# Segment mean: data of the last rows in halves, and looks, ids and counts of the last rows moved forward

## Chip, cores, metric

One core of one Trainium2 chip. The metric is the time of one execution in device microseconds (us). Each ratio below is given with its 95% interval and the chip it was measured on. "Row" is one of 90 slices of 875 values per partition; VectorE is DVE in the profile, ScalarE is ACT, GpSimd is POOL, the sync engine is SP.

## The reference

```python
n = 10_000_000; num_segments = 10000
data = np.random.randn(n).astype(np.float32)
segment_ids = np.sort(np.random.randint(0, num_segments, n))

sums = np.zeros(num_segments); counts = np.zeros(num_segments)
np.add.at(sums, segment_ids, data)
np.add.at(counts, segment_ids, 1)
return sums / np.maximum(counts, 1)
```

The ids are sorted, so a row of one partition holds at most a few segments. The kernel reads a sparse sample of the ids ("probes"), works out per row where the boundary must lie (the "look"), gathers only the 175 ids around it, and from them gets the exact boundary.

## The kernel before

Four engines share a row. GpSimd issues the gathers of a group of six rows after VectorE's look has computed their addresses. ScalarE adds up the gathered ids of a row (`add_ids`, which gives `KK`, the boundary) and the row's data (`total`). VectorE sums the data before the boundary (`split`), and in between does the small work on counts and outputs that `after[r]` holds. The data come in tiles of two rows from the sync engine.

```python
def x_sum(r):                       # how many rows ahead the ids of row r are added
    return 6 if r < HALVES else 3   # HALVES = 66

def load_data(t):                   # tile t = rows 2t and 2t+1, one transfer of 875 KB
    d = dpool.tile([P, 2 * L], FP32, name="data_t")
    a, b = 2 * t * L, min(2 * (t + 1) * L, D)
    c = b if t < NT - 1 else a + L  # only the last tile goes in two transfers
    nc.sync.dma_start(out=d[:, 0 : c - a], in_=data_p[:, a:c])
    if c < b:
        nc.sync.dma_start(out=d[:, c - a : b - a], in_=data_p[:, c:b])

def add_ids(r):                     # ScalarE, KK[r] = sum over 175 ids
    if r >= HALVES:
        nc.scalar.activation(out=junk_a, in_=gt32[:, r % RING, 0 : 2 * W : 2], func=ACT.Identity,
                             scale=-1.0, bias=YY[:, r : r + 1], accum_out=KK[:, r : r + 1])
        if r == NR - 1:             # the correction for the short last row
            nc.scalar.activation(out=KK[:, r : r + 1], in_=KK[:, r : r + 1], func=ACT.Identity, bias=tl)
        return
    ...
def total(r):                       # ScalarE, sum of the row
    nc.scalar.activation(out=junk_t[:, 0:n], in_=d, func=ACT.Copy, accum_out=t_of(r, r + 1))
def split(r):                       # VectorE, sum of the row before the boundary
    nc.vector.scalar_tensor_tensor(out=junk_v[:, 0:n], in0=iota[:, 0:n], scalar=KK[:, r : r + 1], in1=d,
                                   op0=ALU.is_lt, op1=ALU.mult, accum_out=A[:, r : r + 1])
... # cut: looks, windows, keys, tables, checks
put(NR - 4, counts(RM, R2), 99)     # VectorE, 7 small instructions, need KK of rows 72 to 89
put(NR - 1, sums(RM, R2, False) + spread(...) + total_of(add, OUT[:, C2:NO]), 99)

for r in range(-X_PIECE - X_DATA, NR):
    ...
    while r >= -1 and gs < NR and gs <= r + x_sum(gs):
        add_ids(gs)
        gs += 1
    if r >= 0:
        total(r)
        split(r)
        for f in after[r]:
            f()
```

Of the kernel before, what the change touches and what calls it, by code (L numbers as in the profile page):

```python
# [19 lines left out]
L = 875  # L20
S = 175
K = L // S
NR = 90
# [7 lines left out]
X_PIECE = 15  # L31
PIECE = 2
X_DATA = 26
X_LOOK = 9
RING = 18
HALVES = 66
NO = 79
# [5 lines left out]
R2 = NR + 4  # L43
RM = 72
RE = 84
C1, CA, C2 = 41, 64, 50
# [71 lines left out]
def kernel(  # L118
# [6 lines left out]
    nc = tc.nc  # L125
# [15 lines left out]
    ctx.enter_context(tc.manual_schedule())  # L141

    def x_sum(r):
        return 6 if r < HALVES else 3


    pr = cpool.tile([P, NR + 1, K], I64, name="pr")
# [7 lines left out]
    bounds = [0]  # L155
# [10 lines left out]
    def load_data(t):  # L166
        d = dpool.tile([P, 2 * L], FP32, name="data_t")
        a, b = 2 * t * L, min(2 * (t + 1) * L, D)
        c = b if t < NT - 1 else a + L
        nc.sync.dma_start(out=d[:, 0 : c - a], in_=data_p[:, a:c])  # L170
        if c < b:
            nc.sync.dma_start(out=d[:, c - a : b - a], in_=data_p[:, c:b])
        tiles[t] = d
# [9 lines left out]
    def view(ap, dims):  # L183
        return bass.AP(ap.tensor, ap.offset, [list(ap.ap[0])] + dims)
# [90 lines left out]
    def first_look(g):  # L275

        a, b = bounds[g], bounds[g + 1]
        n = b - a
        far = fpool.tile([P, n], FP32, name="far", bufs=3)
        last = b == NR  # L280
        v = nc.vector

        def s1():
            v.tensor_reduce(out=SG[:, a:b], in_=pr32[:, a:b, 0 : 2 * K : 2], axis=AX.X, op=ALU.add)  # L284

        def s2():
            v.scalar_tensor_tensor(  # L287
                out=ST[:, a:b], in0=VI[:, a + 1 : b + 1], scalar=float(K), in1=SG[:, a:b],
                op0=ALU.mult, op1=ALU.subtract,
            )  # L290

        def s3():
            v.tensor_scalar(out=far, in0=ST[:, a:b], scalar1=0.0, scalar2=FAR, op0=ALU.is_equal, op1=ALU.mult)  # L293

        def s4():
            v.tensor_add(out=ST[:, a:b], in0=ST[:, a:b], in1=far)  # L296

        def s5():
            for c, d, w in [(a, b - 1, S), (b - 1, b, TAIL)] if last else [(a, b, S)]:
                v.scalar_tensor_tensor(  # L300
                    out=IDX[:, c:d], in0=ST[:, c:d], scalar=float(w), in1=wb[:, c:d], op0=ALU.mult, op1=ALU.add
                )
            if a < HALVES:
                v.scalar_tensor_tensor(  # L304
                    out=YY[:, a:b], in0=ST[:, a:b], scalar=float(K + 1), in1=SG[:, a:b], op0=ALU.mult, op1=ALU.add
                )
            else:
                v.tensor_add(out=YY[:, a:b], in0=ST[:, a:b], in1=VI[:, a + 1 : b + 1])
            if last:
                v.tensor_scalar(  # L310
                    out=tl, in0=ST[:, NR - 1 : NR], scalar1=-1.0, scalar2=float(TAIL - S),
                    op0=ALU.add, op1=ALU.mult,
                )
            gather(g)

        return [s1, s2, s3, s4, s5]

    def gather(g):
        for r in range(bounds[g], bounds[g + 1]):
            nc.gpsimd.indirect_dma_start(  # L320
                out=GT[:, r % RING, :],
                out_offset=None,
                in_=ids2d[:],
                in_offset=bass.IndirectOffsetOnAxis(ap=IDX[:, r : r + 1], axis=0),
                bounds_check=N - W,
                oob_is_err=False,
            )
# [58 lines left out]
    pb = cpool.tile([P, NO - C2, R2 - RM], FP32, name="pb")  # L386
# [153 lines left out]
    def check_columns():  # L540

        return [
            lambda i=i, q=q, r=r: nc.scalar.activation(
                out=bad[:, NC + 5 + i : NC + 6 + i], in_=VI[:, r : r + 1], func=ACT.Relu, scale=q,
                bias=edge[:, i : i + 1],
            )
            for i, (q, r) in enumerate(((-1.0, R1), (-1.0, RM), (1.0, RM - 1)))
        ]
# [19 lines left out]
    def counts(a, b):  # L568


        n = b - a
        ps = fpool.tile([P, n], FP32, name="ps")
        ct = fpool.tile([P, n], FP32, name="ct")

        def s1():
            nc.vector.tensor_add(out=ps, in0=KK[:, a:b], in1=QQ[:, a:b])  # L576

        def s2():
            nc.vector.tensor_tensor_scan(  # L579
                out=PS[:, a + 1 : b + 1], data0=ps, data1=ps, initial=PS[:, a : a + 1],  # L580
                op0=ALU.max, op1=ALU.max,
            )

        def s3():
            nc.vector.tensor_sub(out=ct, in0=ps, in1=PS[:, a:b])  # L585

        def s4():
            nc.vector.reciprocal(out=ct, in_=ct)  # L588

        def s5():  # L590
            c = min(b, NR)
            nc.vector.tensor_mul(out=RB[:, a:c], in0=BT[:, a:c], in1=ct[:, 0 : c - a])  # L592
            if c < b:
                nc.vector.tensor_mul(out=RB[:, c:b], in0=MX[:, 0 : b - c], in1=ct[:, c - a : n])  # L594

        return [s1, s2, s3, s4, s5]
# [75 lines left out]
    def table(m0, m1, t):  # L672
        def s1():
            nc.vector.tensor_tensor(
                out=sel[:, m0:m1], in0=sel[:, m0:m1], in1=windows(RF, m0, m1), op=ALU.mult
            )

        def s2():
            nc.vector.tensor_reduce(
                out=t[:, 7 * m0 : 7 * m1].rearrange("p (m k) -> p m k", k=7), in_=sel[:, m0:m1],  # L680
                axis=AX.X, op=ALU.add,
            )

        return [s1, s2]

    def place(c0, c1, t, outs):
        def s1():
            n = c1 - c0
            nc.vector.tensor_tensor(
                out=shf[:, c0:c1, 0:ND], in0=view(t[:, c0 : c0 + 1], [[1, n], [1, ND]]),  # L690
                in1=view(dm[:, 0:1], [[0, n], [1, ND]]), op=ALU.mult,
            )

        def s2():
            for a, b, d, o in outs:
                nc.vector.tensor_reduce(out=o, in_=shf[:, a:b, 0:d], axis=AX.X, op=ALU.add)

        return [s1, s2]

    def pick(e, o, c0, n, a, b):  # L700

        w = b - a

        def s1():
            c = min(b, NR)
            e.tensor_scalar(
                out=KL[:, a - R1 : c - R1], in0=VI[:, a:c], scalar1=sp[:, 0:1], scalar2=None, op0=ALU.subtract
            )
            if c < b:
                e.tensor_scalar(  # L710
                    out=KL[:, c - R1 : b - R1], in0=V[:, c:b], scalar1=sp[:, 0:1], scalar2=None,
                    op0=ALU.subtract,
                )

        def s2():
            k, j = view(KL[:, a - R1 : a - R1 + 1], [[0, n], [1, w]]), view(jj[:, c0 : c0 + 1], [[1, n], [0, w]])
            if e is nc.vector:
                e.tensor_tensor(out=o, in0=k, in1=j, op=ALU.is_equal)
            else:
                e.tensor_tensor(out=o, in0=k, in1=j, op=ALU.subtract)  # L720
                e.tensor_scalar(out=o, in0=o, scalar1=0.0, scalar2=None, op0=ALU.is_equal)  # L721

        return [s1, s2]
# [26 lines left out]
    NG = len(GROUPS)  # L750
    NT = (NR + 1) // 2
# [7 lines left out]
    def put(r, steps, every=1):  # L759
        for i, f in enumerate(steps):  # L760
            after[r + i // every].append(f)
# [6 lines left out]
            put(a - 1, second_look(a, b))  # L768
    for g in range(HEAD, NG):
        if g < NG - 1:  # L770
            put(max(bounds[g] - X_LOOK, 0), first_look(g), 5)

    def mixed(p, q):
        out = []
# [8 lines left out]
    def sentinel():  # L783
# [11 lines left out]
    t = table(M1, NT1 // 7, tax)  # L795
# [12 lines left out]
    CF = 7 * H1 - ND + 1  # L808
    put(50, place(0, CF, tab, [(0, CF, ND + 1, OUT[:, 0:CF])]))
    put(65, place(CF, T1, tab, [(CF, C1, ND + 1, OUT[:, CF:C1]), (C1, T1, ND + 1, xa[:, 0 : T1 - C1, RM - R1])]))  # L810
    look = bounds[NG - 1] - X_LOOK - 2
    put(46, check_frame(), 2)
    put(66, check_windows())
    put(65, pick(nc.vector, pa[:, :, 0 : RM - R1], C1, CA - C1, R1, RM))
    put(66, check_columns(), 99)
    put(68, pick(nc.gpsimd, pb[:, :, 0 : RE - RM], C2, NO - C2, RM, RE), 99)
    put(look, first_look(NG - 1), 99)
    put(RM - 3, counts(R1, RM), 2)
    put(look, pick(nc.gpsimd, pb[:, :, RE - RM :], C2, NO - C2, RE, R2), 99)
# [5 lines left out]
    put(RM + 3, spread(R1, RM, pa[:, :, 0 : RM - R1], xa[:, :, 0 : RM - R1], CA - C1, nc.gpsimd)[1:])  # L825
    put(83, total_of(xa[:, 0 : C2 - C1, :], OUT[:, C1:C2])
        + total_of(xa[:, C2 - C1 :, :], add[:, 0 : CA - C2, nb]))
    put(NR - 4, counts(RM, R2), 99)
    put(NR - 1, sums(RM, R2, False) + spread(RM, R2, pb, add[:, :, 0:nb], NO - C2) + total_of(add, OUT[:, C2:NO]), 99)
    assert max(after) <= NR - 1  # L830

    def ahead(p):
        return X_PIECE if p == 0 else p - 1 - 2 * max((p - 4) // 4, (p - X_PIECE - 1) // 2)
# [3 lines left out]
    gs = 0  # L837
    for r in range(-X_PIECE - X_DATA, NR):
        while pnext < NR and pnext <= r + ahead(pnext) + X_DATA:
            n = GROUPS[0] if pnext == 0 else PIECE  # L840
# [4 lines left out]
            pnext += n  # L845
        while nt < NT and 2 * nt <= r + X_DATA:
            load_data(nt)
            nt += 1
        if r == -X_DATA:
            nc.scalar.dma_start(  # L850
# [48 lines left out]
```

## Time and profile before

| | before |
|---|---|
| median of 4 runs | 187.98 us (187.78 to 190.61; the 190.61 was slow) |
| span of the profiled run | 186.0 us |
| busy: VectorE, ScalarE, GpSimd | 137.3, 120.5, 99.2 us |
| bytes moved | 54.62 MB |
| row 84 starts on VectorE | 171.48 us |
| last reduction ends | 181.83 us |

Until about 172 us the transfers are full; from row 84 on VectorE works without a gap. The lines that show this stand in the prediction. In the timeline lines here and below the columns are: start in us, duration in us, engine, line of the program, operation, what it writes and reads, shapes, count, and in brackets the idle time just before with what ended it. VectorE's `junk_v` is a row's split, ScalarE's `junk_t` a row's total, ScalarE's `junk_a` a row's ids.

### The profile page before, as it was taken

Reading aid. Unit: us, or ns where it says so; the run is one execution under the profiler, and the core shown is the slowest. Engines: PE = TensorE matmul, PEld = TensorE weight load, DVE = VectorE, ACT = ScalarE, POOL = GpSimd, SP = SyncE. Lnnn points to the kernel's source line nnn. Section 1 sums busy time; section 2 is a strip of 40 time slices with the busy share of each in tenths; the row PEclk is TensorE's granted clock in tenths of the full one; section 3 lists DMA queues with packets and bytes.
Section 4 is the critical chain, followed back from the end, with each engine's and each line's share of the span. In section 5 each row is a group of like instructions: output and inputs, shape, how many; then the busy total and the mean of one; then the engine's idle time right before and its main releaser. Section 6 shows DMA issues by size and latency. Waiting matters only on the chain. (4 is left out here: it accounts for less than half of the span.)

```text
span 186.0 us, 1471 instructions
## 1 busy us (share of the span) xinstructions
PE 2.2 (1%) x8; PEld 1.9 (1%) x8; DVE 137.3 (74%) x414; ACT 120.5 (65%) x371; POOL 99.2 (53%) x119
## 2 busy tenths in 40 slices
PE   0000000000002000000000000000000000110000
PEld 0000000000001000000000000000000000110000
DVE  7410089999278994955799998766689979887991
ACT  8001487933899186962846939387569769998920
POOL 4677767057843757166173572827517857782000
DMA  6999999999999999999999999999999999999100
GB/s 28 324 250 269 267 283 281 327 333 318 325 321 323 336 331 309 332 327 325 309 297 327 342 319 319 312 306 335 335 286 299 336 351 404 405 399 396 50 0 10
DMA packets 70612, 54.62 MB, mean 294 GB/s; under 512 B 60464, under 2 KB 61032, under 8 KB 70599
## 3 DMA queue, kind: packets, MB, share of 16 engines
q1 hardware_dynamic: 64667, 40.50, 74.6%
q0 software_dynamic: 5760, 14.01, 24.4%
q14 instruction: 13, 0.11, 0.2%
q10 hardware_dynamic: 172, 0.00, 0.1%
HBM read 56.59 MB, written 0.04 MB: 305 GB/s over the span
## 5 line engine op out<-in xcount | busy, mean ns | idle before, releaser
L320 POOL DMA_INDIRECT GT<-in_segment_ids_dram,IDX x90 | 90.0, 1001 | 66.6 <-issue 23.5
L361 DVE SCALAR_TENSOR_TENSOR junk_v<-iota,q,data_t 128x875 bf16<-128x875 f32 x90 | 100.7, 1119 | 16.9 <-DMA data_t<-in_data_dram 14.6
L356 ACT ACTIVATE junk_t<-data_t 128x875 bf16<-128x875 f32 x90 | 83.7, 930 | 10.1 <-DMA data_t<-in_data_dram 9.8
L338 ACT ACTIVATE junk_a<-GT 128x175 f32<-128x175 int32 x66 | 22.1, 334 | 46.6 <-DMA GT<-in_segment_ids_dram,IDX 33.6
L356 ACT ACTIVATION_READ_ACCUMULATOR junk_t<-data_t 128x1 f32 x90 | 15.4, 171 | 0.0
L284 DVE TENSOR_REDUCE SG<-pr 128x6 f32<-128x30 int32 x15 | 2.7, 179 | 15.3 <-DMA pr<-in_segment_ids_dram 15.3
L331 ACT ACTIVATE junk_a<-GT,YY 128x175 f32<-128x175 int32 x24 | 9.9, 412 | 0.0
L338 ACT ACTIVATION_READ_ACCUMULATOR junk_a<-GT 128x1 f32 x66 | 9.3, 141 | 0.0
L361 DVE DVE_READ_ACCUMULATOR junk_v<-iota,q,data_t 128x1 f32 x90 | 7.4, 82 | 0.0
L345 DVE SCALAR_TENSOR_TENSOR q<-YY,G 128x6 f32<-128x6 f32 x11 | 1.7, 156 | 7.2 <-ACT junk_a L338 7.2
L331 ACT ACTIVATION_READ_ACCUMULATOR junk_a<-GT,YY 128x1 f32 x24 | 4.6, 192 | 0.0
L186 ACT ACTIVATE GT<-q 128x3150 int32<-128x3150 f32 x1 | 3.0, 2991 | 0.0
L293 DVE TENSOR_SCALAR far<-ST 128x6 f32<-128x6 f32 x15 | 2.6, 171 | 0.5
L300 DVE SCALAR_TENSOR_TENSOR IDX<-ST,wb 128x6 int32<-128x6 f32 (+2 forms) x16 | 2.6, 165 | 0.5
L287 DVE SCALAR_TENSOR_TENSOR ST<-pr,SG 128x6 f32<-128x6 int32 x15 | 2.5, 166 | 0.5
L296 DVE TENSOR_TENSOR ST<-ST,far 128x6 f32<-128x6 f32 x15 | 2.5, 165 | 0.5
L721 POOL TENSOR_SCALAR pb<-pb 128x348 f32<-128x348 f32 (+1 forms) x2 | 2.1, 1028 | 0.2
L560 PE MATMUL misc<-bads,ones 128*128 128x1 f32 x2 | 0.6, 362 | 102.2 <-ACT badj L552 102.2
L186 ACT ACT_TABLE_LOAD x1 | 1.3, 1283 | 0.7 <-PEq L883 0.7
L304 DVE SCALAR_TENSOR_TENSOR YY<-ST,SG 128x6 f32<-128x6 f32 x11 | 1.7, 158 | 0.0
L560 PEld LDWEIGHTS misc<-bads,ones 128*128 128x128 f32 x2 | 0.5, 310 | 102.3 <-ACT badj L552 102.3
L720 POOL TENSOR_TENSOR pb<-KL,jj 128x348 f32<-128x348 f32 (+1 forms) x2 | 1.5, 733 | 0.2
(126 smaller groups left out, 46.0 us busy)
## 6 DMA issues: line engine op xcount, KB each, us to landing
data_t<-in_data_dram SPq DMA_DIRECT2D x44, 875.0 KB, 10.0
GT<-in_segment_ids_dram,IDX POOLq DMA_INDIRECT x90, 6.3
pr<-in_segment_ids_dram SPq DMA_DIRECT2D x41, 10.0 KB, 7.4
data_t<-in_data_dram SPq DMA_DIRECT2D x1, 437.5 KB, 18.4
data_t<-in_data_dram SPq DMA_DIRECT2D x1, 125.0 KB
out_dram<-OUT SPq DMA_DIRECT2D x1, 36.6 KB
pr<-in_segment_ids_dram SPq DMA_DIRECT2D x1, 31.0 KB, 4.0
snt<-in_segment_ids_dram ACTq DMA_DIRECT2D x1, 1.0 KB
```

The source lines that it names most:

```text
L186: nc.scalar.activation(out=gt32[:, :, 0 : 2 * W : 2], in_=view(q5[:, 0, 0:1], [[0, RING], [0, W]]), func=ACT.Copy)
L284: v.tensor_reduce(out=SG[:, a:b], in_=pr32[:, a:b, 0 : 2 * K : 2], axis=AX.X, op=ALU.add)
L287: v.scalar_tensor_tensor(out=ST[:, a:b], in0=VI[:, a + 1 : b + 1], scalar=float(K), in1=SG[:, a:b], op0=ALU.mult, op1=ALU.subtract,)
L293: v.tensor_scalar(out=far, in0=ST[:, a:b], scalar1=0.0, scalar2=FAR, op0=ALU.is_equal, op1=ALU.mult)
L296: v.tensor_add(out=ST[:, a:b], in0=ST[:, a:b], in1=far)
L300: v.scalar_tensor_tensor(out=IDX[:, c:d], in0=ST[:, c:d], scalar=float(w), in1=wb[:, c:d], op0=ALU.mult, op1=ALU.add)
L320: nc.gpsimd.indirect_dma_start(out=GT[:, r % RING, :], out_offset=None, in_=ids2d[:], in_offset=bass.IndirectOffsetOnAxis(ap=IDX[:, r : r ...
L331: nc.scalar.activation(out=junk_a, in_=gt32[:, r % RING, 0 : 2 * W : 2], func=ACT.Identity, scale=-1.0, bias=YY[:, r : r + 1], accum_out=K ...
L338: nc.scalar.activation(out=junk_a, in_=gt32[:, r % RING, 0 : 2 * W : 2], func=ACT.Copy, accum_out=g_of(r, r + 1),)
L356: nc.scalar.activation(out=junk_t[:, 0:n], in_=d, func=ACT.Copy, accum_out=t)
L361: nc.vector.scalar_tensor_tensor(out=junk_v[:, 0:n], in0=iota[:, 0:n], scalar=KK[:, r : r + 1], in1=d, op0=ALU.is_lt, op1=ALU.mult, accum_ ...
L721: e.tensor_scalar(out=o, in0=o, scalar1=0.0, scalar2=None, op0=ALU.is_equal)
```

## The change

Intent: let each row of the last tiles start when its own data are there, and clear the way for it: looks earlier so that the ids are there, ids five rows ahead, and the counts that need the last ids two rows earlier, so that less stands behind the last data. (`bounds[NG - 1]` is 84.)

```diff
+FINE = 78
     def x_sum(r):
-        return 6 if r < HALVES else 3
+        return 6 if r < HALVES else 3 if r < bounds[NG - 1] else 5
-        c = b if t < NT - 1 else a + L
+        c = b if 2 * t < FINE else a + L
-            put(max(bounds[g] - X_LOOK, 0), first_look(g), 5)
+            put(max(bounds[g] - X_LOOK - 2 * (g == NG - 2), 0), first_look(g), 5)
-    look = bounds[NG - 1] - X_LOOK - 2
+    look = bounds[NG - 1] - X_LOOK - 3
-    put(68, pick(nc.gpsimd, pb[:, :, 0 : RE - RM], C2, NO - C2, RM, RE), 99)
+    put(66, pick(nc.gpsimd, pb[:, :, 0 : RE - RM], C2, NO - C2, RM, RE), 99)
-    put(NR - 4, counts(RM, R2), 99)
+    put(NR - 6, counts(RM, R2), 99)
```

One line added near the top shifts all line numbers by one: L577 after is L576 before, L337 is L336.

## The prediction

> **What bounds the kernel now.** I began with the page's slices, to see which resource is full in which stretch.
>
> ```profile
> DVE  7410089999278994955799998766689979887991
> ACT  8001487933899186962846939387569769998920
> POOL 4677767057843757166173572827517857782000
> DMA  6999999999999999999999999999999999999100
> GB/s 28 324 250 269 267 283 281 327 333 318 325 321 323 336 331 309 332 327 325 309 297 327 342 319 319 312 306 335 335 286 299 336 351 404 405 399 396 50 0 10
> ```
>
> A slice is 4.65 us. The transfers are full from the second slice to the 37th, that is to about 172 us, and no compute engine is full over that time. So the transfers set the pace until 172 us; then VectorE works alone. Moving loads about cannot shorten the first part: the bytes stay the same. What can be won lies in the 14 us behind it, and the chain that ended last says of what they consist:
>
> ```profile
> 173.88 0.09 issue
> 173.98 1.14 DVE junk_v L361 x2
> ...
> 176.33 1.06 DVE junk_v L361 x2
> ...
> 180.98 0.85 DVE OUT L739
> ```
>
> VectorE never pauses here up to 181.83 us; the output transfer takes the rest to 186.0. To find where this unbroken run starts, I read the timeline of the end backwards, counting rows from row 89 (the only one 250 wide, at 178.59 us):
>
> ```profile
> 162.45 1.13 DVE L361 SCALAR_TENSOR_TENSOR junk_v<-iota,q,data_t 128x875 bf16<-128x875 f32 x1 [0.59 <-ACT junk_a L331]
> 165.36 1.13 DVE L361 SCALAR_TENSOR_TENSOR junk_v<-iota,q,data_t 128x875 bf16<-128x875 f32 x1 [0.53 <-DMA data_t<-in_data_dram]
> 168.70 1.13 DVE L361 SCALAR_TENSOR_TENSOR junk_v<-iota,q,data_t 128x875 bf16<-128x875 f32 x1 [0.97 <-DMA data_t<-in_data_dram]
> 171.48 1.13 DVE L361 SCALAR_TENSOR_TENSOR junk_v<-iota,q,data_t 128x875 bf16<-128x875 f32 x1 [0.23 <-ACT junk_a L331]
> 174.20 0.29 ACT L336 ACTIVATE q<-q,tl 128x1 f32<-128x1 f32 x1
> 175.03 0.18 DVE L576 TENSOR_TENSOR ps<-q,QQ 128x22 f32<-128x22 f32 x1
> ```
>
> These are rows 78, 80, 82 and 84, each the first of a two-row tile, each behind an idle gap; then ScalarE's last id instruction (row 89) and the start of the last counts. The trace's completion records put the ends of these four tiles at about 162.4, 165.23, 168.58 and 171.35 us, just before each start. So I read the two gaps charged to ScalarE as waits for data as well: ids of rows 78 and 84 were added three rows earlier. From row 84 at 171.48 there is no gap. **The time is therefore the start of row 84 plus a fixed run of work of 10.35 us (to 181.83) plus the output**, and the start of row 84 is the arrival of rows 84 and 85 together.
>
> **What the Trainium skill says.** "DMA: Bandwidth & Descriptors", section "Anatomy of one DMA — SWDGE (gpsimd) path", says that a transfer's semaphore can't fire until its last byte has landed. The starts 0.05 to 0.13 us after the four completions agree: row 84 waits for row 85's bytes too. The same page, "Specifications", asks for at least 512 B per transfer for line rate. The halves have 3500 B per partition: in the trace the packets of that size (the last tile, split already) took a median 139 ns, those of 7000 B 268 ns, so 25.2 against 26.1 B/ns, 4% less in packets that are few. The same page, "Issuing engines are not separate DMA queues", has all transfers interleave on the same 16 engines; so an earlier gather takes bandwidth from data that flow at that time. The trace agrees as far as it goes: the slices stay near 400 GB/s with gathers and data mixed.
>
> **The change, part by part.**
>
> *Data row by row from row 78.* Five tiles go in two halves each; five more issues on the sync queue, at about 0.33 us each where nothing blocks them (the last half-tile's issue took 0.33 us). That queue seems to hold at most eight transfers in flight: the second half of the last tile was issued at 159.26 us, when the transfer eight before it (rows 76 and 77) landed at about 159.3. Eight halves are 3.5 MB, an estimated 8.8 us of the 400 GB/s, so the queue does not run dry. The first row of each tile can now start half a tile sooner. For row 84: 437.5 KB (448,000 B) at 400 GB/s are 1.12 us, so its half lands at about 171.35 - 1.12 = 170.2 instead of 171.35. VectorE has to be free: the second half of rows 82/83 lands at about 168.6 to 168.9, row 83 runs 1.13 us plus about 0.1, and the small reduction of 0.25 us behind it ends near 170.1 to 170.4. So row 84 starts at about 170.3: 171.48 - 170.3 = 1.2 us sooner, 1.0 if the tile before is late. Of the wait at rows 80 and 82 (0.53 and 0.97 us) nothing more comes through, since the arrival of row 84 caps it.
>
> *Looks ahead.* The look for rows 78 to 83 moves from row 69 to row 67, that for rows 84 to 89 from 73 to 72. The work is the same (about 1.0 us of small VectorE instructions each). GpSimd's mask work (0.35 + 0.78 + 1.09 us) now stands before row 67 in the program, but it already ran at 146.12 to 148.52, right after the previous gathers. Then it waited 1.68 us for the look. With the look at about 145.5 to 146.5 us that wait goes: the first gather starts at 148.8 instead of 150.20, 1.4 us sooner. The twelve follow at 1.30 us each, the last at about 163.2 instead of 164.63. With 6.7 us to landing (median in this stretch), ids of row 89 are there at 169.9 instead of about 171.3. The price: 1.4 us x 138 GB/s (179 KB per 1.30 us) = 0.19 MB of gathers ahead of the data, so rows 74 to 83 arrive up to 0.5 us later. It is paid back when the gathers end sooner, at about 170.3; the arrival of row 85, behind all of them, stays near 171.35.
>
> *Last counts behind row 84.* Seven small instructions, from 175.03 to 176.25, 1.1 us net of what overlaps. They move from behind row 86 to behind row 84; this is a pure swap in a stretch without gaps and earns nothing in itself. But they need the ids of row 89, including the correction at L336.
>
> *Ids 5 rows ahead from row 84.* It is there to serve that need. ScalarE's order decides: ids of 83, 84, 85 fall before the sum of row 80, then 86, 87, 88, 89 before the sums of 81 to 84. From the timeline ScalarE takes 0.89 us for a row's sum and 0.43 for a row's ids in steady work (164.89, 165.32, 166.21, 166.64). It stood at 169.98 before the sum of row 83 with ids up to 86 done, including 0.7 us of waiting for rows 82/83; without that 169.3. Add one sum and the ids of 87 and 88: 169.3 + 0.89 + 0.86 = 171.05 is the start of ids 89; plus 0.86 to the end of the correction (173.63 to 174.49 in the trace) gives **171.9**. If rows 76/77 come 0.5 us late, everything behind shifts: 172.4.
>
> VectorE reaches the counts at 170.3 + 1.28 + 0.1 = 171.65 (row 84 and the small reduction behind it, the 1.28 being the spacing of rows 84 and 85). So it waits 0.25 us in the good case and 0.75 in the bad one. Sum: 1.0 to 1.2 us gained on row 84's start, less 0.25 to 0.75 for the ids: 0.25 to 0.95 us, middle 0.6. From 188.09 that is 187.5.
>
> **The rivals.**
>
> *The ids become the bound.* A new wait in front of the counts eats the whole gain if row 89's count is ready only at about 172.7 (before, row 85 started at 172.76; with the counts in front that equals 172.7 + 1.1 = 173.8, which is 172.76 plus the 1.1 moved). For it: the sum above has only 0.3 to 0.8 us to spare, and seven gathers (83 to 89) each land only about a microsecond before ScalarE wants them. Against: GpSimd's pace is steady at 1.30 us. It would make 188.0 to 188.5.
>
> *No such wait, full gain.* If the data of rows 76/77 come no later and ScalarE loses no time between its rows, the gain is the 1.2 us of the first half: 186.9. VectorE would then be without a gap from 170.3, and 1.2 us is the ceiling, as the bytes before row 84 cannot come sooner.
>
> *The split is hidden or harmful.* Halves could come out of order or at a lower rate, or take a smaller share beside the gathers, so that row 84 still starts after 171.2. The 4% longer packets over ten rows would cost at most 0.04 x 5 x 2.24 us = 0.45 us (2.24 us being one tile at 400 GB/s), and only if the engines are that inefficient while overlapped. Time 188.0 to 188.5. I give this little weight since slices with a mix of 1400 to 4200 B gathers already run at 400 GB/s.
>
> *A large win or loss.* A large win would need less traffic or less VectorE work at the end; neither changes. A large loss needs a stall of several microseconds, for instance a look that waits for its first ids. The last of those landed at about 153.3 us and the look for rows 84 to 89 would come at about 154.2, so 0.9 us are to spare.
>
> **Range and chances.** The sum gives 187.1 to 187.8, the rivals 186.9 to 188.5. The three runs before spread from 187.86 to 190.61, the two lower ones 0.2 apart, so a median of few runs adds some 0.2 to either side. I take 186.8 to 188.3, lying more below the old time than above. Two per cent are 3.76 us, three times the ceiling of the gain; only a slow execution or an unseen stall could leave the band.
>
> **What would show it.** In the profile after: row 84 starting at 170.2 to 170.5 with the gaps before rows 80 and 82 gone or halved; the first gather of rows 78 to 83 directly behind GpSimd's mask work, near 148.8; the correction at L336 ending near 172, and a gap of 0.2 to 0.8 us in front of L576 on VectorE that names ScalarE; from there no gap, and L739's last reduction ending near 181.2. The slices of GB/s at the end unchanged within a few per cent. I am wrong if row 84 still starts after 171, if L336 ends later than 172.7, if the sync queue shows gaps in the transfers before 170 us, or if VectorE waits again behind row 85.

## The result, and the profile after

188.47 us median of 4 runs (188.26 to 188.84) against 187.98 before, ratio 1.0032, interval 1.0007 to 1.0056. Executions over 1.5% slower than the fastest of the same kernel are left out of the means. A ratio is always the mean time of one kernel's fast runs over that of the other's of the same rounds, so not quite the ratio of the medians. The prediction of 187.5 with a range of 186.8 to 188.3 missed: the gain of 0.5 us did not come, and the median lies 0.17 us above the range.

The slices of the changed kernel, as before 4.65 us each:

```profile
DVE  7410089999277994855899999586879979877791
ACT  8002387942979386964837939287759787979930
GB/s 28 326 260 264 266 281 286 325 332 320 330 323 327 327 330 307 336 330 322 311 309 330 328 318 332 326 329 312 324 294 352 332 360 388 393 383 373 16 0 10
```

The transfers end slightly sooner (16 instead of 50 GB/s in the 38th slice) and are about as fast as before, so no large part was lost there. VectorE's digits at the end are lower (8 7 7 7 9 instead of 8 8 7 9 9), although its work is the same: it has gaps where it had none. The timeline of the changed kernel from row 84 on shows them; in order: row 84, ScalarE's correction for row 89, the first instruction of the counts, row 85, the last reduction.

```profile
169.82 1.13 DVE L362 SCALAR_TENSOR_TENSOR junk_v<-iota,q,data_t 128x875 bf16<-128x875 f32 x1
172.54 0.29 ACT L337 ACTIVATE q<-q,tl 128x1 f32<-128x1 f32 x1
172.87 0.18 DVE L577 TENSOR_TENSOR ps<-q,QQ 128x22 f32<-128x22 f32 x1 [1.69 <-ACT q L337]
174.09 1.12 DVE L362 SCALAR_TENSOR_TENSOR junk_v<-iota,q,data_t 128x875 bf16<-128x875 f32 x1
181.17 0.85 DVE L740 TENSOR_REDUCE OUT<-add 128x29 f32<-128x667 f32 x1
```

Row 84 starts at 169.82 instead of 171.48, with no gap in front: 1.66 us won, more than predicted. Then VectorE stands still for 1.69 us in front of the counts until ScalarE has finished row 89's ids, and the last reduction ends at 182.02 instead of 181.83. What was won at row 84 was given back one step later.

The correction was predicted to end at 171.9; it ended at 172.83. Looking back along ScalarE, these four lines are the ids of row 81, the total of row 78, the ids of row 82 and the total of row 79; the last line below is row 79 on VectorE.

```profile
161.74 0.41 ACT L332 ACTIVATE junk_a<-GT,YY 128x175 f32<-128x175 int32 x1
162.17 0.92 ACT L357 ACTIVATE junk_t<-data_t 128x875 bf16<-128x875 f32 x1
163.05 0.41 ACT L332 ACTIVATE junk_a<-GT,YY 128x175 f32<-128x175 int32 x1
164.70 0.93 ACT L357 ACTIVATE junk_t<-data_t 128x875 bf16<-128x875 f32 x1 [1.12 <-ACT junk_a L332]
162.67 1.13 DVE L362 SCALAR_TENSOR_TENSOR junk_v<-iota,q,data_t 128x875 bf16<-128x875 f32 x1
```

ScalarE pauses for 1.12 us before the total of row 79, although VectorE had begun on the same half tile 2.0 us earlier. So it is not a wait for the data. The profile names ScalarE itself as what ended the pause; that name alone would not exclude something else. The trace's semaphore records say a little more: ScalarE's own check for the data of row 79 stands at 162.60, the read of the accumulator for the ids of row 82 ended at 163.58, and the next count of ScalarE's own semaphore is recorded at 164.68, 0.02 us before the total began. Whether that count came late or was only recorded late they don't say. This pause was in nobody's sum.

A simple sum holds in every trace in which the counts stand behind row 84: **end of the last reduction = start of row 84 + 10.52 us + gap before the counts**. Here 169.82 + 10.52 + 1.69 = 182.03 (182.02 measured). Before, the fixed part was 10.35 without a gap. The experiments are read by the two terms, the start of row 84 and the gap.

### The profile page after: what moved, and what is told of

Its sections match the earlier page's. It is cut to its first block, busy times and chain, and to the rows that moved or that the text cites. A ratio compares the mean times of both kernels' runs of the same rounds, so it can differ in the third digit from the quotient of the medians.

```text
span 186.1 us, 1481 instructions
## 1 busy us (share of the span) xinstructions
PE 2.2 (1%) x8; PEld 1.9 (1%) x8; DVE 137.1 (74%) x414; ACT 121.0 (65%) x371; POOL 99.5 (53%) x119
## 4 chain that ended last, share of the span: by engine, by line
DMA 42%; issue 21%; ACT 14%; SPq 8%; DVE 8%; POOL 4%; DVEq 1%; ACTq 0%; POOLq 0%
DMA data_t<-in_data_dram 24%; DMA GT<-in_segment_ids_dram,IDX 15%; ACT junk_t L357 8%; SPq L171 6%; DVE junk_v L362 5%; POOL GT L321 4%; ACT junk_a L332 3%; DMA pr<-in_segment_ids_dram 3%; SPq L163 3%; ACT junk_a L339 2%; DVEq L285 1%; DVE OUT L740 0%; DVE add L732 0%; DVE PS L580 0%; ACT badj L553 0%
## 5 line engine op out<-in xcount | busy, mean ns | idle before, releaser
L577 DVE TENSOR_TENSOR ps<-q,QQ 128x44 f32<-128x44 f32 (+3 forms) x4 | 0.7, 178 | 1.7 <-ACT q L337 1.7
```

## The experiments

My theory after the first trace (A): the counts wait for row 89's ids, and that is the whole loss. Rivals: ScalarE's totals are the next bound (B); the halves or looks cost something elsewhere (C). All runs gave the reference's result unless said otherwise. Each group of runs is on one chip, with its own runs of the kernel before.

### Group 1 (chip 11): parts undone, and the changed kernel again

`e1_counts_back`, the changed kernel with
```diff
-    put(NR - 6, counts(RM, R2), 99)
+    put(NR - 4, counts(RM, R2), 99)
```

> The changed kernel with one part undone: the last counts stand behind row 86 again; data in halves, looks and ids 5 rows ahead stay. Theory A (the wait for row 89's ids in front of the counts is the whole loss): row 84 starts near 169.8 us as in the changed kernel and the 10.35 us of work behind it run without a gap, so VectorE ends near 180.2 and the time is about 186.4. Theory B (ScalarE's own row sums are the next bound: the last ended at 178.33 in the changed kernel): the gap before the counts is gone, but the final sums wait for ScalarE until about 178.4, and the time is about 187.2. Theory C (the halves or the looks cost something elsewhere): 188.0 or more.

`e2_ids3`, e1 and in addition
```diff
-        return 6 if r < HALVES else 3 if r < bounds[NG - 1] else 5
+        return 6 if r < HALVES else 3
```

> Halves and looks of the change only: counts behind row 86 and ids 3 rows ahead throughout, as before. ScalarE then takes ids and sums in strict turns (in the traces an id step after a sum and a sum after an id step cost 1.31 us together, two id steps in a row 0.57 each, two sums in a row 1.03 each), so its last sum should end about 0.6 us sooner than with 5 ahead. Theory A: about 186.4, as e1. Theory B: 186.6 to 186.9, that is 0.3 to 0.6 us below e1. If the counts now wait for row 89's ids, a gap of up to 0.5 us stands in front of them.

`e3_halves_only`, the kernel before with
```diff
-        c = b if t < NT - 1 else a + L
+        c = b if 2 * t < FINE else a + L
```

> The kernel before with the halves alone; looks, counts and ids as before. The gathers then come 2.7 us later than in the changed kernel (last issued at 164.63 against 161.96). If the halves alone bring the gain (theory A): row 84 starts near 170.0 and the time is 186.5 to 187.0. If the earlier looks are needed for it, because ScalarE then waits for ids of rows 84 to 89 (landed at 165.5 to 172.3 in the trace before): ScalarE's sums end no sooner than before (177.9), VectorE waits for the ids in front of the counts, and the time is 187.5 to 188.

`e4_again`, the changed kernel unaltered.

> The changed kernel unaltered, for a second trace and a tight interval: ScalarE stood still for 1.12 us before the sum of row 79 in the first trace although that row's data had landed 2 us earlier for VectorE. If that pause belongs to the kernel, it is there again and the gap before the counts is again near 1.7 us, time 188.5. If it was a mishap of one execution, row 89's ids are ready about 1.1 us sooner, the gap is near 0.6 us and the time of that run near 187.3.

Measured against the kernel before on this chip (mean of its ten fast runs 188.61 us): e1 0.9981 (0.9939 to 1.0023), e2 0.9962 (0.9928 to 0.9996), e3 0.9949 (0.9910 to 0.9988), e4 0.9943 (0.9898 to 0.9988). The changed kernel, unaltered, is faster than before here: median of its fast runs 187.35. Its second trace has no pause on ScalarE; in the order of the first such fence, row 84, correction, counts, row 85, last reduction:

```profile
170.29 1.13 DVE L362 SCALAR_TENSOR_TENSOR junk_v<-iota,q,data_t 128x875 bf16<-128x875 f32 x1
171.63 0.29 ACT L337 ACTIVATE q<-q,tl 128x1 f32<-128x1 f32 x1
171.96 0.18 DVE L577 TENSOR_TENSOR ps<-q,QQ 128x22 f32<-128x22 f32 x1 [0.30 <-ACT q L337]
173.19 1.12 DVE L362 SCALAR_TENSOR_TENSOR junk_v<-iota,q,data_t 128x875 bf16<-128x875 f32 x1
180.26 0.85 DVE L740 TENSOR_REDUCE OUT<-add 128x29 f32<-128x667 f32 x1
```

This is the prediction's trace almost to the digit: row 84 at 170.29 (170.3), correction done at 171.92 (171.9), gap 0.30 (0.25), time of this run 187.35 (187.5). So the sum was right for this execution, and the pause is no fixed property of the program. (e5 below, also nearly without a pause, does not meet the sum.)

Theory A's forecast for e1 (186.4) missed by 2 us (the kernel before is itself 0.6 us slower on this chip than in the first runs). The gap before the counts is gone, but the profiled run of e1 took 189.13, because its row 84 started at 172.17: in it rows 80, 81, 82 and 86 waited 1.26, 0.52, 0.16 and 0.45 us, late data as far as the profile names a cause. e2 and e3 lie near e4, not near 186.4. Theory B fell as well: in e1 to e3 the last totals end at 176.8 to 178.7, before VectorE's final sums begin (178.1 to 180.2). Theory C's general slowdown did not show on this chip. The halves alone (e3) are as fast as the whole change (e4) here.

### Group 2 (chip 2): a third trace, the wait longer, the halves undone, the wait taken away

`e5_after_third`, the changed kernel unaltered.

> The changed kernel unaltered, a third trace. In the second one the pause of 1.12 us on ScalarE before the sum of row 79 was absent, the gap before the counts was 0.30 us and the time 187.35. Theory P (the pause is a mishap of the one execution, and the change itself gains about 0.3 to 0.6%): no pause here, gap 0.2 to 0.6 us, ratio to the kernel before of 0.994 to 0.998. Theory Q (pause or no pause comes with the chip or the session, and the kernel is no faster): pause again or gap above 1.2 us, ratio 1.000 to 1.005.

`e6_counts83`
```diff
-    put(NR - 6, counts(RM, R2), 99)
+    put(NR - 7, counts(RM, R2), 99)
```

> The suspected wait made longer on purpose: the last counts behind row 83 instead of 84, nothing else changed. They then stand on VectorE one row (1.23 us) earlier while row 89's ids are ready when they are. If the time follows that wait one for one, the gap in front of the counts is about 0.3 + 1.25 = 1.5 us, row 84 follows behind the counts, and the time is about 1.2 us above that of the changed kernel in this call, so about that of the kernel before (ratio 0.998 to 1.003). If the wait is hidden by other waits (data of rows 84 and 85), less than 0.5 us is lost.

`e7_no_halves`
```diff
-FINE = 78
+FINE = 88
```

> The changed kernel with the halves undone (only the last tile split, as before); looks, counts behind row 84 and ids 5 ahead stay. If the halves are what gains: row 84 starts near 171.4 as in the kernel before, row 89's ids are ready near 171.9 and so before the counts want them, no gap there, and the time equals that of before within 0.3%. If looks and ids gain by themselves, it lies nearer to the changed kernel (ratio 0.995).

`e8_counts85`
```diff
-    put(NR - 6, counts(RM, R2), 99)
+    put(NR - 5, counts(RM, R2), 99)
```

> The counts behind row 85 instead of 84, the rest as changed: takes away the wait for row 89's ids without touching data or ScalarE. By the prediction's sum it gains the whole of that wait: 0.3 us below the changed kernel of this call, VectorE without a gap from row 82 on, time near 187.0 in an execution like the second one. If the pause of the first trace comes again it still costs nothing up to 1.3 us. If the counts were no part of the path: no difference to the changed kernel.

Measured: e5 1.0054 (1.0019 to 1.0089), e6 0.9991 (0.9955 to 1.0026), e7 1.0075 (1.0026 to 1.0124), e8 1.0010 (0.9975 to 1.0045). On this chip the changed kernel is slower than before, clear of noise. Theory P's ratio was wrong here; Theory Q's (1.000 to 1.005) was right but for 0.0004, though its gap of over 1.2 us was not: e5 had 0.94 us and hardly a pause (0.1 us), and row 84 started at 171.22 because rows 74 and 76 had already started 0.8 and 1.3 us later than in the second trace.

e6 gave a wrong result (relative error 0.024) and is no test of what it was built for. Behind row 83 the counts stand in the program before the ids of row 89, so they read the old value of that row and wait for row 88's ids only. It was a mistake in the design of the run. Its one use: with a wait for an earlier id the gap was 1.12 us, still ScalarE.

e8 against e5 is the clearest result of the group: the counts one row later, ratio lower by 0.44%, 0.8 us, where 0.3 was forecast. The two intervals overlap; from five runs of each I estimate the difference at 0.1 to 1.6 us, so it is just clear of noise. In its trace ScalarE is as late as in the others (it finished row 89 at 173.11), and the counts start at 173.16 without a gap. So the gap before the counts is on the path, and a row between serves as a cushion. The end of the trace moves by 1.38 us, of which 0.94 is the gap and 0.38 an earlier row 84.

e7 was to show what the halves are worth. Row 84 started at 170.54, not at 171.4, and there was a gap of 1.09 us: the forecast that ids would be in time without halves was wrong, because ScalarE paused again. The time missed too: 0.75% above before, where 0.3% at most was forecast, and no better than e5, so what the halves are worth on this chip stays open. These are the total of row 78, the ids of row 82 and the total of row 79 in e7:

```profile
162.10 0.92 ACT L357 ACTIVATE junk_t<-data_t 128x875 bf16<-128x875 f32 x1
163.42 0.42 ACT L332 ACTIVATE junk_a<-GT,YY 128x175 f32<-128x175 int32 x1 [0.34 <-ACT junk_t L357]
164.83 0.94 ACT L357 ACTIVATE junk_t<-data_t 128x875 bf16<-128x875 f32 x1 [0.86 <-ACT junk_a L332]
```

In e7 rows 78 and 79 are one transfer, which ScalarE was already using for row 78 at 162.10. So the 0.86 us before row 79 cannot be a wait for data.

### Group 3 (chip 13): a hold-up of known size, before and after

From here the theory is S: the change did not make ScalarE slower, it spent the slack that had swallowed its hold-ups. `e9_before_again` and `e11_after_fourth` are the two kernels unaltered; in `e10_before_pause` and `e12_after_pause` each has

```diff
+            if r == 79:
+                nc.scalar.activation(out=junk_t, in_=tiles[39][:, L : 2 * L], func=ACT.Copy)
             total(r)
```

> The kernel before, unaltered, for a second trace of it on the chip of the next three runs. Theory S (the change spent ScalarE's slack: before, a hold-up of ScalarE around rows 76 to 82 is swallowed by its wait for the data of rows 82 and 83, 0.62 us, and by 0.54 us between its correction for row 89 and the counts; after, it goes into the time one for one): whatever pauses ScalarE has here, VectorE has no gap before the counts and row 84 starts within 0.1 us of its data. Theory T (pauses only come with the changed order of instructions): no pause on ScalarE here, though the changed kernel on the same chip has one. Ratio 1.00 by construction.

> The kernel before with a hold-up of known size: one more copy of row 79's data on ScalarE (0.92 us, its result unused) in front of the sum of row 79. Theory S: swallowed, ratio to the kernel before 0.999 to 1.002, no gap before the counts. If ScalarE was as tight before as after: about 1.0 us more, ratio 1.005.

> The changed kernel unaltered, a fourth trace. By the sum that held in the three traces so far (start of row 84 + 10.5 us + gap before the counts = end of the last reduction, within 0.05 us) its end is again given by these two terms. A chip like the one of the second trace (no pause): ratio 0.994 to 0.997; a chip with pauses: 1.002 to 1.006.

> The changed kernel with the same hold-up of 0.92 us on ScalarE in front of the sum of row 79. Theory S: the correction for row 89 ends about 1.0 us later, the gap before the counts grows by as much, and the time is 0.8 to 1.1 us above that of the changed kernel of this call (ratio higher by 0.0045 to 0.006). If the gap is swallowed elsewhere: under 0.3 us.

Measured: e9 1.0002 (0.9966 to 1.0038), e10 1.0055 (1.0006 to 1.0104), e11 1.0027 (0.9993 to 1.0062), e12 1.0075 (1.0044 to 1.0106).

e9 shows that the kernel before has pauses too, so theory T fell: here before the total of row 81, whose tile row 80 had already used. The other lines are the correction and the counts.

```profile
166.75 0.94 ACT L356 ACTIVATE junk_t<-data_t 128x875 bf16<-128x875 f32 x1 [0.62 <-ACT junk_a L331]
173.56 0.29 ACT L336 ACTIVATE q<-q,tl 128x1 f32<-128x1 f32 x1
174.39 0.18 DVE L576 TENSOR_TENSOR ps<-q,QQ 128x22 f32<-128x22 f32 x1
```

The correction ends at 173.85, the counts start at 174.39 without a gap: the pause cost nothing. In the changed kernel the hold-up came through. e12, the extra copy and then the correction and the counts:

```profile
164.53 0.94 ACT L866 ACTIVATE junk_t<-data_t 128x875 bf16<-128x875 f32 x1
173.80 0.29 ACT L337 ACTIVATE q<-q,tl 128x1 f32<-128x1 f32 x1
174.13 0.18 DVE L577 TENSOR_TENSOR ps<-q,QQ 128x22 f32<-128x22 f32 x1 [1.66 <-ACT q L337]
```

e12 is 0.48% slower than e11, 0.9 us, within the forecast of 0.8 to 1.1. Its trace does not follow the forecast: the correction ended at 174.09, not 1.0 us later than in e11 but 0.39 sooner, and the gap grew by 0.55 us instead of 1.0; e11's trace ran later as a whole (row 84 by 0.94 us). And e10 missed: 0.55% slower than before where at most 0.2% was expected; 1.005 was the forecast for a ScalarE as tight before as after. Its trace has a pause of 1.24 us of its own behind the copy, so ScalarE lost 1.0 + 1.24 us against a slack of 0.62 + 0.54, and a gap of 0.64 us stood in front of the counts. That could mean slack for one hold-up and not for two, but of the 2.42 us by which e10's trace ends later than e9's, 1.69 are a later row 84 (row 76 was already 1.6 us later), and only 0.64 the gap. So the contrast that theory S promised is not there: the same copy cost 0.9 us after the change and 1.0 before it (the latter, from five runs of each, is by my estimate -0.3 to 2.3). That a hold-up was swallowed is seen once, in the trace of e9; theory S is not shown.

### Group 4 (chip 8): halves and looks apart

`e13_halves_again` is e3, `e14_ids3_again` is e2, `e16_after_fifth` the changed kernel, and `e15_looks_only` is e2 with

```diff
-FINE = 78
+FINE = 88
```

> The halves alone, as in e3, on another chip. If counts and ids moved forward are the loss (theory S): no gap before the counts, or under 0.3 us, and faster than the kernel before by 0.6 to 1.2 us (ratio 0.994 to 0.997), below the changed kernel of this call. If the halves themselves do not pay on such a chip (theory H): ratio 0.999 to 1.004, as bad as the changed kernel.

> Halves and looks, counts behind row 86, ids 3 ahead, as e2. Theory S: as fast as e13, 0.6 us or more below the changed kernel (e16) of this call. If the earlier looks cost (theory L: gathers ahead of the data of rows 74 to 77): row 76 starts 0.3 to 0.5 us later than in e13 and the time is 0.2 to 0.5 us above e13.

> The earlier looks alone, no halves, counts and ids as before. Theory L: rows 74 to 77 get their data 0.3 to 0.5 us later than in the kernel before and nothing is won at row 84: ratio 1.000 to 1.004. Otherwise the same as before within 0.2%.

> The changed kernel unaltered, for comparison within this call. A chip with pauses: gap before the counts of 0.9 us or more, ratio 1.002 to 1.006; without: gap of 0.3 us, ratio 0.994 to 0.997.

Measured: e13 1.0030 (0.9992 to 1.0069), e14 1.0008 (0.9963 to 1.0052), e15 1.0026 (0.9993 to 1.0059), e16 1.0054 (1.0005 to 1.0104). The order of e14, e13 and e16 is that of theory S, with intervals that overlap, but none is faster than before, so "the halves alone pay" fell as a general statement: on this chip they do not. e16 had a gap of 0.46 us, between its two forecasts. In e13 ScalarE paused 2.85 us before the ids of row 83, whose gather had moved its last bytes by 161.82 us (with `remote` the profile names no instruction or transfer that ended the pause), and the gap before the counts was 1.92 us even with the counts behind row 86:

```profile
167.13 0.42 ACT L332 ACTIVATE junk_a<-GT,YY 128x175 f32<-128x175 int32 x1 [2.85 <-remote]
```

Theory L was not confirmed by e15: its ratio lies in the forecast range, but its row 76 started at 159.21 (159.48 and 159.13 in the two unaltered traces of before). Nor by e14: row 76 came 2.9 us later than in e13 (161.94 against 159.00) where 0.3 to 0.5 was forecast, yet its ratio is the lower one. In kernels with both halves and looks rows 74 to 77 tend to come late: row 76 starts on average at 160.1 us in their eleven traces up to here (158.93 to 161.94), at 159.3 in the seven others (158.76 to 160.73). The ranges overlap, and I did not isolate it.

### Group 5 (chip 8): is the pause a place in the instruction stream?

The pauses had all come at ScalarE's 458th to 471st record, shortly after an 8 KB transfer of the instruction queue (162.6 to 165.0 us in those traces). `e17_shift16` and `e18_shift32` put 16 and 32 tiny copies in front, while ScalarE waits for its first ids:

```diff
+    pad = cpool.tile([P, 16], FP32, name="pad")       # 32 in e18
+    for i in range(16):
+        nc.scalar.activation(out=pad[:, i : i + 1], in_=q5[:, 0, 0:1], func=ACT.Copy)
```

> The changed kernel with 16 tiny copies on ScalarE in front, while it waits for its first ids (from 5 to 13 us), so each later instruction of it has a number higher by 16. If the pauses belong to a place in the instruction stream (theory F): the pause, if this chip has one, stands again at records 458 to 471, which is now 2 to 2.5 rows earlier, before the instructions of rows 76 or 77, and the instruction transfer that was at 162.6 to 165.6 us comes 3 us earlier. If they belong to the algorithm or to the moment (theory M): still between the sums of rows 78 and 81. A trace without a pause tells neither. Time: 0.5 us or less from the changed kernel.

> The same with 32 copies. Theory F: pause at records 458 to 471, now four to five rows earlier (rows 74 to 75), where ScalarE waits for data anyway, so that it costs less, and the instruction transfer comes about 6 us earlier than 162.6 to 165.6. Theory M: still between the sums of rows 78 and 81. Time: if a pause of about 1 us is gone from the path, up to 1 us below the changed kernel (ratio 0.996 to 1.000), otherwise 1.002 to 1.006.

Measured: e17 1.0003 (0.9966 to 1.0040; its profile fell into a slow run, 191.0 us), e18 0.9998 (0.9954 to 1.0043). The pause did not move with the count. In e17 it stands before the total of row 79, record 477, in e18 before the ids of row 82, record 490, that is 461 + 16 and 458 + 32; one line of each:

```profile
167.44 0.94 ACT L360 ACTIVATE junk_t<-data_t 128x875 bf16<-128x875 f32 x1 [1.36 <-ACT junk_a L335]
```

```profile
164.54 0.42 ACT L335 ACTIVATE junk_a<-GT,YY 128x175 f32<-128x175 int32 x1 [0.77 <-ACT junk_t L360]
```

Meanwhile the instruction transfer had moved to 161.54 and 153.62 us, as forecast for theory F. So theory F fell: the pause does not follow the place in the instruction stream or its transfer. For e17 that is the reading of a slow run; e18 alone says the same. The forecasts of the time missed: e18 kept its pause and a gap of 1.45 us, yet measured 0.9998 where 1.002 to 1.006 was expected in that case.

The record holds a rival that I did not test: **the recording of the profile itself**. The traces are of two kinds. In five (the first of before and the four of chip 11) 3,740 to 3,822 updates of semaphores are recorded; from 163 to 168 us ScalarE stands still in them for over 0.15 us only where the profile names a transfer. In the other fifteen 2,312 to 2,604 are recorded, and thirteen of them have a pause of 0.2 us or more between 163 and 168 us for which no transfer is named. In eleven of the thirteen it ends within 0.1 us of the end of a stretch with few records. In the first trace of the changed kernel 30 updates and landings of transfers are recorded from 160 to 165 us and 232 from 165 to 170; the total of row 79 starts at 164.70. Nor does such a pause belong to rows 78 to 81: in that trace there are 21 records from 50 to 55 us and 152 from 55 to 60, and

```profile
55.61 0.94 ACT L357 ACTIVATE junk_t<-data_t 128x875 bf16<-128x875 f32 x1 [1.02 <-ACT junk_a L339]
```

Six more of the fifteen have one between 54 and 58 us, the five denser traces none. This is a coincidence in time, not a proof; no run without recording is on record, so whether the pauses would be there without it stays open.

### The traces side by side

| run (chip) | kernel | start of row 84 | gap before counts | sum | measured end |
|---|---|---|---|---|---|
| first trace | before | 171.48 | 0 | +10.35 = 181.83 | 181.83 |
| e9 (13) | before | 170.84 | 0 | 181.19 | 181.19 |
| first trace | changed | 169.82 | 1.69 | +10.52 = 182.03 | 182.02 |
| e4 (11) | changed | 170.29 | 0.30 | 181.11 | 181.11 |
| e5 (2) | changed | 171.22 | 0.94 | 182.68 | 182.67 |
| e11 (13) | changed | 172.04 | 1.11 | 183.67 | 183.67 |
| e16 (8) | changed | 172.19 | 0.46 | 183.17 | 183.17 |
| e7 (2) | changed, no halves | 170.54 | 1.09 | 182.15 | 182.16 |
| e12 (13) | changed, hold-up | 171.10 | 1.66 | 183.28 | 183.28 |

All in us. The two terms give the end of each trace within 0.01 us. The constants 10.35 and 10.52 were read from the first trace of before and from e4; the other rows test them.

## Why the prediction was wrong

**What bounds the kernel: right as far as it went.** The end is the start of row 84 plus fixed work plus the gap before the counts, in all nine traces above. Two sums are slightly off without effect: 170.3 + 1.28 + 0.1 is 171.68, and eight halves are 3.58 MB, 9.0 us. The gathers came as predicted, directly behind GpSimd's mask work: the first one of rows 78 to 83 on average 1.4 us sooner in the traces with the earlier looks.

**Row 84 about 1.2 us sooner: right for the first trace and e4 (1.66 and 1.19 us), too sure in general.** Over the five traces of the changed kernel row 84 starts between 169.82 and 172.19 us, 171.1 on average, no sooner than in the two traces of the kernel before. The halves did what they were to do: from the start of row 76 to that of row 84 the changed kernel takes 10.5 to 11.2 us, before 12.0 and 11.7. But in three of the five traces row 76 itself started at 160.7 to 161.2 instead of 159.1 to 159.5. The prediction let rows 74 to 83 come up to 0.5 us late and said "It is paid back when the gathers end sooner". It was not paid back.

**"So it waits 0.25 us in the good case and 0.75 in the bad one": this is the step that failed.** The gap was 1.69 us in the trace of the result and 0.90 on average over the five. The prediction's own sign of being wrong, the correction ending after 172.7, came true. In that trace ScalarE started row 76 at 158.89, 0.44 sooner than the sum assumed, so row 89 should have been ready at 171.46; it was ready at 172.83, 1.37 later. Of that 1.12 is the pause before row 79 and 0.28 are two ids in a row: the sum took 0.43 us for each, but ids behind ids start 0.57 apart (165.59, 166.15, 166.73 in that trace), 0.43 only from ids to a total. e4 shows the size of the term without the pause: 0.30. It is not the pause alone: e5 had 0.94 with hardly one, because ScalarE's row 76 came 1.46 us later than in e4 and VectorE's row 84 only 0.93. I had named "the ids become the bound" as a rival at 188.0 to 188.5; that is what the result shows, and the range should have reached that far.

**"A pure swap" of the counts: 0.17 us too cheap.** The fixed part grew from 10.35 to 10.52. In exchange the counts fill a gap: in e1 and e2, with halves and the counts behind row 86, row 86 waited 0.45 us.

**The rivals.** Harmful halves: not in general (e3 0.9949), but not excluded on a chip like that of e13 (1.0030). Full gain: never seen. No large loss: right.

**What the chips make of it.** The changed kernel measured 1.0032, 0.9943, 1.0054, 1.0027 and 1.0054 of before, mean 1.0022. The one chip where it wins is the one whose traces have no such pause; there the ids were in time. It is also the one whose traces hold the many records. That the pauses decide between the chips is argued, not shown: e5 and e16 are slow almost without a pause, through late data. What stays open is what the pauses are, and whether the recording makes them. Shown is that in the first trace of the changed kernel, e7 and e17 the data were there, and that they do not move with ScalarE's instruction count. No other version was run on all chips; the most promising is e8, run on one of them, counts behind row 85, 0.8 us below the changed kernel of its group and level with the kernel before.

## What to carry to other kernels

A transfer wait taken off the path can come back as the next wait: in the first trace row 84 came 1.66 us sooner and the counts then waited 1.69 us for their ids. Leave a row of other work between a consumer and its producer where it costs nothing (e8, 0.8 us). That a consumer moved closer feels each hold-up one for one, and the kernel before did not, was my theory and is not shown. Before believing half a per cent, run both kernels on several chips: one trace of one chip would have "proved" a gain here, another a loss. When a sum of two terms fits every trace, read the failures by its terms instead of by the total. And before explaining a pause in a trace, compare how many records the traces hold.

## What the Trainium skill lacked or had wrong

- "DMA: Bandwidth & Descriptors", "Anatomy of one DMA — SWDGE (gpsimd) path", says that a semaphore fires after the last byte (written there for GpSimd's path; the tiles here come from the sync engine). In the trace of before 15 of the 16 completions of the tile of rows 82 and 83 fell between 165.34 and 166.91 us and the last at 168.58, so the tile's arrival is that of one late engine of the sixteen. In e4 a half tile spread as much (163.19 to 166.14), a later one only from 167.29 to 167.82: halving did not by itself make the spread smaller.
- The same page, "Issuing engines are not separate DMA queues", gives no number for how gathers in front delay other data. Here row 76 started on average 0.8 us later in kernels with both halves and earlier gathers, more than the bytes of 1.4 us of gathers account for (0.5 us), and not later with earlier gathers alone (159.21 and 158.86 us in e15 and e7). The ranges overlap, so this is a hint.
- "ScalarE: Activation LUTs" has nothing on accumulating instructions in a row. Here ids after a total cost 0.43 us and a total after ids 0.89, but two ids in a row 0.57 each and two totals 1.03 each, so strict turns save 0.29 us per pair.
- "Perfetto Trace Analysis" does not say that a trace can lack records, nor that pauses like ScalarE's (0.21 to 2.85 us here) may come with that. Five traces held 3,740 to 3,822 semaphore updates, fifteen 2,312 to 2,604 for nearly the same program; in those the profile often names "issue" or the engine itself where a transfer may have been meant.
